# Hybrid GLA, FoX and memory block: the token norm of x moved from the activations to where projections leave PSUM

## The chip, the cores and the metric

The kernel runs on one core of a Trainium2 chip. The metric is the device time of one execution in microseconds; the figure given is the median of the runs. The engines are named as in the profile: PE is TensorE's matmul, PEld its weight load, DVE is VectorE, ACT is ScalarE, POOL is GpSimd, SP is SyncE, which issues most DMAs.

## The reference

x is 512 tokens of 1024 channels, mem 256 tokens of 1024; all is float32. One layer is computed:

```
u    = rmsnorm(x, g_mix)                 # x * rsqrt(mean(x^2) + eps) * g, per token
proj = u @ w_in                          # GLA q,k,v,gate,low-rank alpha | FoX q,k,v,forget | memory query | 3 x 1024 gates
log_a = log_sigmoid(ga @ w_alpha_up + b_alpha) / 16
o_gla = rmsnorm(gla_chunk_causal(gq/8, gk, gv, log_a), g_gla_head) * silu(gg)
o_fox = softmax(fq @ fk.T / 8 + F_t - F_s, causal) @ fv      # F = cumsum(log_sigmoid(ff + b_forget))
mk, mv = split(rmsnorm(mem, g_mem) @ w_mem_kv)
o_mem = softmax(mq @ mk.T / sqrt(128)) @ mv
merged = sum over branches of sigmoid(gate) * (o @ w_o)
h = x + merged @ w_out
h = h + relu(rmsnorm(h, g_ffn) @ w_ff1)^2 @ w_ff2
out = rmsnorm(h, g_final)
```

The norm of a token is one number, so it can be applied to u before a projection or to the projection's result.

## The kernel before, in words

Every large product is made in three matmuls: each factor is split into a high part (a cast to fp32r, on ACT) and a low part (the difference, on DVE), and `mm3` (L150) adds hi x hi, hi x lo and lo x hi in PSUM. The stationary factor is 128x128; the moving one has 512 columns, or 256 for mem. Weights come in chunks of 128x1024 in the order of `chunk_list`; `get_w` (L147) loads one on SP's queue (L136, tile raw, three buffers), casts whi (L142) and subtracts wlo (L143), three buffers each. Every second chunk also starts a DMA on POOL's queue that prepares sums of later weights (`next_sum`, L120).

`gT` (L155) is a projection with channels on partitions: eight steps of three matmuls, k over the 1024 input channels, result 128x512 in one PSUM bank, handed to an evacuation function. `gN` (L165) is a projection with tokens on partitions. Both are generators, so that `weave` (L188) can put steps of one stage as fill between steps of another. PE's order is the order of the program text; the other engines' orders are written by a scheduler at build time.

The front (L267 to L370): mem is loaded transposed, with channels on partitions, scaled by g_mem and split into mxh and mxl. The first five weight chunks are loaded and split by `lead` (L274). Four key projections of mem follow (`mk_proj`, L336), then the value projection of mem (L355, `gN`, sixteen steps). Meanwhile ACT squares mem and x, POOL and DVE add the squares over the channel slices (`sq_cols`, L206), and PE sums them over partitions with a column of ones (`rms_cols`, L218, matmuls at L224). `rsqrt` (L227) makes the norms per token: the mean on DVE, the power on POOL (L231). `bcast_rows` (L234) lays a norm out along the free axis for all partitions: ACT makes diagonal matrices (L239), PE multiplies them by ones (L240), ACT copies the result (L241). x's row rxb is then multiplied into each slice of x (L365 on POOL, L367 on DVE), and the product is split into uhi and ulo (L368). u_end is the last of these.

After the front come: G, a projection of the 16 alpha and 8 forget columns (L388); FoX queries and keys of the first head pair (`fox_pair`, L438); `decay_logs` (L396) and `decay_sums` (L408) on G's result, with FoX values as fill; the second pair; eight FoX heads (`fox_scores`, `fox_turn`, `fox_values`) woven with the other FoX and GLA projections; memory attention (L607 to L664) woven with the first gate branch; GLA (L669 to L792) woven with the second; then the third gate branch, the output projection, and from about 530 us the MLP.

`branch` (L578) makes for each of eight column blocks a gate projection, its tanh (L583) straight from PSUM, four product steps, and a combination on DVE (L596, L598). In memory attention the query of head 0 is projected first (L658); each round of the woven list then holds values of head h-2, transposes of h-1, the query projection of h+1 and scores of h, in this order. Query splits qh and ql have two buffers.

## Time and profile before

| | us |
|---|---|
| median of 3 runs | 866.18 (865.49 to 867.07) |
| profiled execution: span of its instructions | 862.5 |
| profiled execution: a time of its own beside the span | none given; the median lies 3.7 above the span |
| PE busy, and share of the span | 839.0, 97% |
| DVE busy | 542.4, 63% |
| ACT busy | 440.3, 51% |
| POOL busy | 113.0, 13% |
| mean DMA rate | 165 GB/s |

The profile is one execution. A row of the timeline gives the start in us from the span's start, the length in us, engine, line, operation, result and operands, shape, count, and in brackets the idle time before it and what ended that. A row of a stretch gives for each engine the busy time and the number of instructions, then PE's granted clock as a share of full speed, the DMA engines' busy share and GB/s. Matmul records overlap, since a matmul's last columns drain while the next one runs; the time from start to start is what a matmul costs in a dense stretch.

### The profile page before, as it was taken

What the parts mean: (1) busy time and instruction counts of PE and PEld (TensorE: products, weight loads), DVE (VectorE), ACT (ScalarE), POOL (GpSimd) and SP (SyncE); (2) the same over time, 40 slices, a digit from 0 to 9 for tenths busy, and PEclk for the clock granted to TensorE, in tenths of its full rate; (3) what the DMA queues carried; (4) which work ended last, traced back from release to release, by engine and by line L of the source; (5) the groups of instructions that cost most, each with busy time, mean ns of one, the idle gap of its engine ahead of it and who ended that gap; (6) DMA issues with size and microseconds to landing.
All of it is one profiled execution on the core that took longest, in us unless ns stands there. A gap on an engine that the chain in (4) does not pass through costs nothing.

```text
span 862.5 us, 11811 instructions
## 1 busy us (share of the span) xinstructions
PE 839.0 (97%) x4513; PEld 711.2 (82%) x4513; DVE 542.4 (63%) x850; ACT 440.3 (51%) x703; POOL 113.0 (13%) x130
## 2 busy tenths in 40 slices
PE   8999999999999999999999999999999999999993
PEld 6778788888888888787888889888997899799872
DVE  5784656756444546474533547675688678778954
ACT  7764746754333432321332436565676377457744
POOL 5100000000000021221112100111001000100234
PEclk9999999999999999999999999999999999999997
DMA  8444745544547355336222413758757956785694
GB/s 320 145 150 168 201 135 178 146 171 123 171 133 230 125 150 168 97 113 231 98 98 98 170 50 118 225 124 204 243 171 162 265 199 171 179 256 176 138 170 133
DMA packets 37513, 142.37 MB, mean 165 GB/s; under 512 B 4592, under 2 KB 5392, under 8 KB 35728
## 3 DMA queue, kind: packets, MB, share of 16 engines
q1 hardware_dynamic: 27216, 93.36, 30.5%
q0 software_dynamic: 8448, 45.09, 24.8%
q10 hardware_dynamic: 1792, 3.16, 1.1%
q8 instruction: 35, 0.57, 0.3%
q14 instruction: 22, 0.18, 0.1%
HBM read 136.34 MB, written 27.28 MB: 190 GB/s over the span
## 4 chain that ended last, share of the span: by engine, by line
PE 74%; issue 12%; DMA 6%; DVE 3%; ACT 2%; POOL 1%; SPq 0%; POOLq 0%; ACTq 0%; DVEq 0%
PE mm L152 20%; PE mm L153 20%; PE mm L151 20%; DMA b<-in_wst_dram 6%; PE a L151 2%; PE a L152 2%; PE a L153 2%; ACT hi L203 1%; PE a L748 1%; DVE lo L204 1%; PE a L477 1%; DMA cst_s<-in_cst_dram 1%; PE a L765 1%; PE a L508 1%; PE a L507 1%
## 5 line engine op out<-in xcount | busy, mean ns | idle before, releaser
L143 DVE TENSOR_TENSOR wlo<-raw,whi 128x1024 fp32r<-128x1024 f32 x80 | 101.7, 1275 | 104.1 <-ACT whi L142 103.5
L142 ACT CAST whi<-raw 128x1024 fp32r<-128x1024 f32 x80 | 84.1, 1053 | 132.3 <-PE mm L152 100.3
L151 PE MATMUL mm<-uhi,whi 128*128 128x512 f32 x360 | 142.5, 396 | 0.0
L152 PE MATMUL mm<-ulo,whi 128*128 128x512 f32 x360 | 140.7, 391 | 1.4 <-DVE ulo L204 1.4
L153 PE MATMUL mm<-uhi,wlo 128*128 128x512 f32 x360 | 140.5, 390 | 0.0
L203 ACT CAST hi<-raw 128x1024 fp32r<-128x1024 f32 x58 | 60.5, 1048 | 44.7 <-PE mm L152 31.7
L204 DVE TENSOR_TENSOR lo<-raw,hi 128x1024 fp32r<-128x1024 f32 x58 | 70.6, 1222 | 17.6 <-ACT hi L203 17.6
L152 PEld LDWEIGHTS mm<-ulo,whi 128*128 128x128 f32 x360 | 67.7, 188 | 15.8 <-DVE ulo L204 2.9
L153 PEld LDWEIGHTS mm<-uhi,wlo 128*128 128x128 f32 x360 | 67.6, 188 | 14.6 <-DVE wlo L143 0.4
L151 PEld LDWEIGHTS mm<-uhi,whi 128*128 128x128 f32 x360 | 67.7, 188 | 13.5 <-issue 0.7
L204 DVE TENSOR_TENSOR lo<-b,hi 128x1024 fp32r<-128x1024 f32 x40 | 48.9, 1223 | 38.3 <-ACT hi L203 38.2
L203 ACT CAST hi<-b 128x1024 fp32r<-128x1024 f32 x40 | 41.9, 1048 | 57.5 <-PE mm L153 24.1
L152 PE MATMUL mm<-lo,ch 128*128 128x512 f32 x160 | 63.4, 396 | 2.5 <-DVE lo L204 2.5
L151 PE MATMUL mm<-hi,ch 128*128 128x512 f32 x160 | 63.1, 395 | 0.9 <-ACT hi L203 0.8
L153 PE MATMUL mm<-hi,cl 128*128 128x512 f32 x160 | 63.0, 394 | 0.0
L1050 POOL DMA_DIRECT2D b<-in_wst_dram x32 | 27.7, 865 | 267.1 <-DVE lo L204 210.2
L152 PE MATMUL mm<-u2l,hi 128*128 128x256 f32 x192 | 54.3, 283 | 0.0
L153 PE MATMUL mm<-u2h,lo 128*128 128x256 f32 x192 | 54.3, 283 | 0.0
L151 PE MATMUL mm<-u2h,hi 128*128 128x256 f32 x192 | 54.3, 283 | 0.0
L151 PE MATMUL mm<-u2sh,hi 128*128 128x256 f32 x144 | 40.8, 283 | 0.0
L152 PE MATMUL mm<-u2sl,hi 128*128 128x256 f32 x144 | 40.8, 283 | 0.0
L153 PE MATMUL mm<-u2sh,lo 128*128 128x256 f32 x144 | 40.8, 283 | 0.0
(349 smaller groups left out, 1945.5 us busy)
## 6 DMA issues: line engine op xcount, KB each, us to landing
raw<-in_wst_dram SPq DMA_DIRECT2D x122, 512.0 KB, 4.0
b<-in_wst_dram POOLq DMA_DIRECT2D x32, 512.0 KB, 5.3
T<-in_wst_dram POOLq DMA_DIRECT2D x12, 1024.0 KB, 8.4
raw<-T SPq DMA_DIRECT2D x24, 512.0 KB, 4.5
b<-in_wst_dram SPq DMA_DIRECT2D x16, 512.0 KB, 5.1
xr<-in_xT_dram SPq DMA_DIRECT2D x4, 512.0 KB, 8.1
nFb<-dF ACTq DMA_DIRECT2D x8, 256.0 KB, 3.8
h<-in_xN_dram SPq DMA_DIRECT2D x4, 512.0 KB, 7.6
```

Of the source, the lines that this page charges most:

```text
L142: cast = nc.scalar.copy(hi, raw)
L143: nc.vector.tensor_tensor(lo, raw, f(hi), op=ALU.subtract)
L151: nc.tensor.matmul(ps, lh, rh, start=start, stop=False)
L152: nc.tensor.matmul(ps, lh, rl, start=False, stop=False)
L153: nc.tensor.matmul(ps, ll, rh, start=False, stop=stop)
L203: nc.scalar.copy(hi, src)
L204: return nc.vector.tensor_tensor(lo, src, f(hi), op=ALU.subtract).ins
L477: nc.tensor.matmul(ps[:, :w], q, K[e][:, 1, :w], start=False, stop=True)
L507: nc.tensor.matmul(po[:, q0:], vv, PTh[:, c0:c0 + w], start=n == 0, stop=False)
L508: nc.tensor.matmul(po[:, q0:], vv, PTl[:, c0:c0 + w], start=False, stop=n == 3)
L748: nc.tensor.matmul(ps[:, t, :], kk[:, sl], qq[:, sl], start=True, stop=True)
L1050: nc.gpsimd.dma_start(to, x, accum_op=ALU.add)
```

## The change

- uhi and ulo are made from x times g_mix, without the token norm. The row rxb lives on through the layer, and every projection's result is multiplied by it (tokens along the free axis) or by the column rtok (tokens on partitions) where it leaves PSUM: G, FoX q, k and v, GLA q, k, v and gate, and the 24 gate blocks. The memory query is split unscaled; its scores take the norm in the softmax's scale (rpos) and maximum (rneg).
- The sums of squares are taken from copies of x and mem in token order, loaded on POOL's queue after the last split of mem: two of mem, four of x, 512 KB each, through two buffers (nat). ACT squares and sums in one instruction, or DVE does. `sq_cols` and `rms_cols` are gone. The broadcast of mem's norm stands after six of the value steps, that of x's norm after four of the eight steps of G.
- The first key projection is a plain f32 product of unsplit weights (w0) with unsplit mem times g_mem (mg); mxh and mxl are made from mg.
- Three small constants are made on POOL instead of DVE; key evacuations of mem go to DVE.
- In FoX a strip of the tile ab is used for scaled results (ev_t) and another for th. In memory attention qh and ql have one buffer, and scores of h stand ahead of the query projection of h+1.

The diff, cut to its core:

```diff
@@ rsqrt: takes r; sq_cols and rms_cols removed @@
+    rtok, rneg, rpos = (cst_s[:, 4 * P + 8 * i:4 * P + 8 * i + NT] for i in range(3))
...
+    rxb = up.tile([P, S], F32, name="rxb")
@@ front @@
+        mg = [sg[k // 2][:, (k % 2) * M:(k % 2) * M + M] for k in range(KT)]
+        def lead(key, tag):
+            raw = (wp if tag == "raw" else fp).tile([P, 1024], F32, tag=tag, name=nm("raw"), bufs=3 if tag == "raw" else 2)
+            pre[key] = [wp.tile([P, 1024], F32R, tag=g, name=nm(g)) for g in ("hi", "lo")]
+            nc.sync.dma_start(raw, wst[index[key]])
+            split(*pre[key], raw)
...
+        w0 = wp.tile([P, 1024], F32, tag="raw", name=nm("raw"))
         for j in range(4):
             nc.sync.dma_start(memr[:, 2 * j:2 * j + 2], memT[:, 2 * j:2 * j + 2])
+            nc.sync.dma_start(w0[:, 256 * j:256 * j + 256], wst[0][:, 256 * j:256 * j + 256])
             for k in (2 * j, 2 * j + 1):
-                nc.scalar.mul(mxh[:, k, :], memr[:, k, :], gmem[:, k:k + 1])
-                nc.vector.scalar_tensor_tensor(mxl[:, k, :], memr[:, k, :], gmem[:, k:k + 1], f(mxh[:, k, :]),
-                                               op0=ALU.mult, op1=ALU.subtract)
-                if k == 2 * j:
-                    lead(chunks[0], 4, j)
+                nc.vector.tensor_scalar(mg[k], memr[:, k, :], gmem[:, k:k + 1], None, op0=ALU.mult)
+            for k in (2 * j, 2 * j + 1):
+                last_mx = nc.scalar.copy(mxh[:, k, :], mg[k])
+                nc.vector.tensor_tensor(mxl[:, k, :], mg[k], f(mxh[:, k, :]), op=ALU.subtract)
...
+        def natural(src, to, on_act):
+            nat = fp.tile([P, D], F32, tag="nat", name=nm("nat"), bufs=2)
+            d = nc.gpsimd.dma_start(nat, src)
+            tc.add_manual_dep(d.ins, last_mx.ins.name, ..., reason="pace")
+            if on_act:
+                nc.scalar.activation(nat, nat, AF.Square, accum_out=to)
+            else:
+                nc.vector.tensor_tensor_reduce(out=nat, in0=nat, in1=nat, scale=1.0, scalar=0.0, op0=ALU.mult, op1=ALU.add,
+                                               accum_out=to)
+        for t in range(2):
+            natural(memN[t * P:(t + 1) * P, :], msum[:, t:t + 1], True)
+        rm = rsqrt(fp, msum, 1.0 / D, 2)
...
         for k in range(KT):
-            sq_cols(fp, memr, M, k, macc, range(KT), "m")
+            nc.scalar.mul(uhi[:, k, :], xr[:, k, :], gmix[:, k:k + 1])
+            u_end = nc.vector.scalar_tensor_tensor(ulo[:, k, :], xr[:, k, :], gmix[:, k:k + 1], f(uhi[:, k, :]),
+                                                   op0=ALU.mult, op1=ALU.subtract).ins
+        nc.gpsimd.tensor_copy(ident16, ident)
+        nc.gpsimd.tensor_scalar(cmask, tri, -1.0, -NEG, op0=ALU.add, op1=ALU.mult)
+        msk_end = nc.gpsimd.tensor_copy(msk_s.rearrange("p a b -> p (a b)"), cst_s[:, 4 * P:6 * P])
+        for t in range(NT):
+            natural(xN[t * P:(t + 1) * P, :], xsum[:, t:t + 1], t % 2 == 0)
+        rsqrt(fp, xsum, 1.0 / D, NT, rtok)
+        nc.vector.tensor_scalar(rpos, rtok, float(P) ** -0.5, None, op0=ALU.mult)
+        nc.vector.tensor_scalar(rneg, rtok, -float(P) ** -0.5, None, op0=ALU.mult)
...
+        ps = mmt()
+        for k in range(KT):
+            nc.tensor.matmul(ps[:, :M], w0[:, k * P:(k + 1) * P], mg[k], start=k == 0, stop=k == KT - 1)
+        nc.vector.tensor_copy(mk_raw(0), ps[:, :M])
+        for h in range(1, 4):
+            mk_proj(h)
+        mv = gN([("N", "w_mem_kv", 2 * j, 512) for j in range(4)], of(mxh, mxl), 2, mmt, mv_evac)
+        run(islice(mv, 6))
         bcast_rows(fp, rm, M, rmb)
-        mk_proj(3)
...
-        rx = rms_cols(fp, xacc, S)
...
-        bcast_rows(fp, rx, S, rxb)
-        for k in range(KT):
-            ut = fp.tile([P, S], F32, tag="ut", name=nm("ut"), bufs=3)
-            if k in UP:
-                nc.gpsimd.tensor_tensor(ut, xr[:, k, :], rxb, op=ALU.mult)
-            else:
-                nc.vector.scalar_tensor_tensor(ut, xr[:, k, :], gmix[:, k:k + 1], rxb, op0=ALU.mult, op1=ALU.mult)
-            u_end = split(uhi[:, k, :], ulo[:, k, :], ut)
         run(mv)
+        g_steps = gT(("G",), uhi, ulo, lambda ps: ga_evac(ps))
+        run(islice(g_steps, 4))
+        bcast_rows(fp, rtok, S, rxb)
@@ FoX and GLA projections @@
-            nc.scalar.copy(gaT, ps)
+            nc.vector.tensor_tensor(gaT, ps, rxb, op=ALU.mult)
...
+        abf = ab.rearrange("p t c -> p (t c)")
+        ev_t, th_t = abf[:, 0:S], abf[:, S:2 * S]
+        def scaled(to, ps, c=None):
+            if c is None:
+                nc.vector.tensor_tensor(to, ps, rxb, op=ALU.mult)
+            else:
+                nc.vector.scalar_tensor_tensor(to, ps, c, rxb, op0=ALU.mult, op1=ALU.mult)
...
             def q_evac(ps):
+                scaled(ev_t, ps, 0.125)
                 for e, a, b in rows:
-                    nc.scalar.mul(Q[a, e, :], ps[a], 0.125)
-                    nc.vector.scalar_tensor_tensor(tq[a], ps[a], 0.125, f(Q[a, e, :]), op0=ALU.mult, op1=ALU.subtract)
+                    nc.scalar.copy(Q[a, e, :], ev_t[a])
+                    nc.vector.tensor_tensor(tq[a], ev_t[a], f(Q[a, e, :]), op=ALU.subtract)
             def k_evac(ps):
+                scaled(ev_t, ps)
                 for e, a, b in rows:
-                    split(K[e][a, 0, :], K[e][a, 1, :], ps[a])
+                    split(K[e][a, 0, :], K[e][a, 1, :], ev_t[a])
...
-            return proj(OFF["gk"] + P * j, lambda ps: nc.scalar.copy(gkT[j], ps))
+            return proj(OFF["gk"] + P * j, lambda ps: scaled(gkT[j], ps))
@@ gates @@
-            nc.scalar.activation(th, ps, AF.Tanh, scale=0.5)
+            nc.vector.tensor_tensor(th, ps, rxb, op=ALU.mult)
+            nc.scalar.activation(th, th, AF.Tanh, scale=0.5)
@@ memory attention @@
-                st["q", h] = [ap.tile([P, S], F32R, tag=g, name=nm(g), bufs=2) for g in ("qh", "ql")]
+                st["q", h] = [ap.tile([P, S], F32R, tag=g, name=nm(g)) for g in ("qh", "ql")]
...
-                nc.vector.tensor_scalar(m2, m2, -sc, None, op0=ALU.mult)
+                nc.vector.tensor_tensor(m2, m2, rneg[:, 2 * g:2 * g + 2], op=ALU.mult)
...
-            for fn, i in ((mem_values, h - 2), (mem_turn, h - 1), (lambda i: run(mem_q(i)), h + 1), (mem_scores, h)):
+            for fn, i in ((mem_values, h - 2), (mem_turn, h - 1), (mem_scores, h), (lambda i: run(mem_q(i)), h + 1)):
```

95 lines of the change are left out of this document (28 added, 67 removed).

## The prediction

> **What bounds the kernel now.** I read first the page's busy shares and the table of stretches of 20 us, then the PE timeline and the waits of the one region where TensorE is not full, and last single rows of the places further on that the change touches.
>
> ```profile
> span 862.5 us, 11811 instructions
> PE 839.0 (97%) x4513; PEld 711.2 (82%) x4513; DVE 542.4 (63%) x850; ACT 440.3 (51%) x703; POOL 113.0 (13%) x130
> ...
> 0.00:20.00 20.00, 16.11 (x79) 11.42 (x80) 10.91 (x18) 15.70 (x35) 10.54 (x15) 0.91 0.87 312
> 20.00:40.00 20.00, 19.04 (x113) 16.52 (x113) 15.02 (x19) 14.24 (x25) 2.97 (x4) 1.00 0.49 173
> 40.00:60.00 20.00, 18.64 (x79) 14.06 (x78) 17.33 (x27) 11.84 (x21) 2.04 (x3) 1.00 0.35 121
> 60.00:80.00 20.00, 20.00 (x91) 16.26 (x90) 8.74 (x23) 11.73 (x17) 1.23 (x2) 1.00 0.52 185
> ```
>
> In the stretches, the second number after each start is TensorE's (PE's) busy time. PE is busy 97% of the span, and from 60 us on it is full. The first 60 us lack 20.00 - 16.11, 20.00 - 19.04 and 20.00 - 18.64, together 6.2 us, and busy time there hides more, since matmuls overlap. So two things can move the time: how soon PE gets through the front, and any new wait in the full part, where a stall of PE costs its whole length.
>
> The front on PE, from the timeline (start, length, line, operands; in brackets the idle time before and who ended it):
>
> ```profile
> 14.34 0.58 PE L153 MATMUL mm<-mxh,lo 128*128 128x256 f32 x1
> ...
> 24.46 0.39 PE L151 MATMUL mm<-hi,mxh 128*128 128x512 f32 x1
> 25.55 0.50 PE L152 MATMUL mm<-lo,mxh 128*128 128x512 f32 x1 [0.69 <-DVE lo L284]
> 26.82 1.84 PE L224 MATMUL a<-cst_s,acc 128*128 128x1 f32 x16
> 28.52 0.49 PE L151 MATMUL mm<-hi,mxh 128*128 128x512 f32 x1
> 32.07 0.60 PE L240 MATMUL a<-dg,cst_s 128*128 128x128 f32 x4
> ...
> 33.48 0.48 PE L151 MATMUL mm<-whi,mxh 128*128 128x512 f32 x1
> ...
> 39.73 0.39 PE L151 MATMUL mm<-uhi,whi 128*128 128x512 f32 x1
> ...
> 42.90 0.50 PE L152 MATMUL mm<-ulo,whi 128*128 128x512 f32 x1 [0.74 <-DVE ulo L204]
> ```
>
> At 14.34 the second key projection for mem begins to flow, at 24.46 the value projection for mem, at 26.82 the sums of squares of x by matmul (1.70 us to 28.52), at 32.07 the broadcast of x's norm (1.41 us to 33.48), at 39.73 the chunk called G, the first to read u. From 33.48 to 39.73 stand nine steps of three matmuls, 6.25 us: 0.231 us each. The row at 42.90 shows what G waits for: ulo, which comes only after norm, product and split of each slice of x.
>
> **The change part by part.** The sum is made against the profiled execution. The profile gives its span, 862.5 us, and no other time of its own; the median, 866.18, lies 3.7 us above, which I take as unchanged launch and end.
>
> *The norm leaves u's path.* The eight products with the norm (L367, L365) go; uhi and ulo are made straight from x, which is long in SBUF, while the mem projections run. G has eight steps, 24 x 0.231 = 5.5 us. The first matmul of the next projection:
>
> ```profile
> 47.50 0.40 PE L151 MATMUL mm<-uhi,whi 128*128 128x512 f32 x1
> ```
>
> From 39.73 to 47.50 it took 7.8 us, so 2.2 us go. What hides the eight casts and eight subtractions is the stretch 24 to 40, where the other engines have room:
>
> ```profile
> 12.00:16.00 4.00, 3.31 (x14) 3.02 (x15) 3.95 (x4) 3.70 (x8) 3.44 (x3) 0.58 1.03 416
> 16.00:24.00 8.00, 8.00 (x69) 8.00 (x69) 4.42 (x6) 6.96 (x14) 3.78 (x4) 1.00 1.01 394
> 24.00:40.00 16.00, 15.04 (x80) 12.52 (x79) 11.38 (x16) 10.56 (x18) 2.38 (x3) 1.00 0.37 119
> ```
>
> (Columns: PE, PEld, DVE, ACT, POOL, then PE's granted clock, DMA share, GB/s.) Beside 16.0 us VectorE (DVE) has 11.4 and ScalarE (ACT) 10.6. If that cover were gone, G would stall as now.
>
> *Sums of squares on PE go:* 1.7 us for x, and for mem a quarter as many instructions, 0.4 us. The broadcast of the norm stays (1.4 us), only later, among G's steps. G is long enough to cover the copy of the row to SBUF.
>
> *The first key projection* becomes eight plain f32 products without a split. It waits on loads as before; I cost it at nothing. The next projection waited at 14.34 for its lo part:
>
> ```profile
> 12.20 3.75 DVE L284 TENSOR_TENSOR lo<-raw,hi 128x256 fp32r<-128x256 f32 x3
> 6.11 0.73 POOL L216 TENSOR_TENSOR acc<-acc,sq 128x256 f32<-128x256 f32 x1 [4.84 <-ACT sq L215]
> 12.40 5.39 POOL L216 TENSOR_TENSOR acc<-acc,sq 128x256 f32<-128x256 f32 x4 [0.61 <-ACT sq L215]
> 23.20 1.04 ACT L283 CAST hi<-raw 128x1024 fp32r<-128x1024 f32 x1
> ```
>
> Three subtractions took 3.75 us while GpSimd (POOL) added squares, four of them 5.39 us, 1.35 each, where one at 6.11 took 0.73. Two engines that stretch each other here no longer meet; I take 0.6 us for it, between 0 and 1.1. The clock of 0.58 from 12 to 16 us (the row above) may stay; were it 1.00, 4 x 0.42 = 1.7 us would be won. I keep that for the lower end. The sum of the gains: 2.2 + 1.7 + 0.4 + 0.6 = 4.9 us.
>
> *New loads in a full stretch.* Two copies of mem and four of x in token order, 0.52 MB each, 3.1 MB, go out on POOL's queue. From 12 to 24 us the DMA share is about 1.0 at 394 to 416 GB/s: there the copies of mem alone cost 1.05 MB / 0.41 = 2.6 us to whatever queues beside them. That is:
>
> ```profile
> 9.23 0.33 SPq L282 DMA_DIRECT2D raw<-in_wst_dram  x1
> 11.26 0.43 SPq L282 DMA_DIRECT2D raw<-in_wst_dram  x1
> 11.74 0.43 SPq L315 DMA_DIRECT2D cst_s<-in_cst_dram  x1
> DMA to landing us min/median/max: 5.1/5.9/7.2
> xr<-in_xT_dram SPq DMA_DIRECT2D x4, 512.0 KB, 8.1
> b<-in_wst_dram POOLq DMA_DIRECT2D x32, 512.0 KB, 5.3
> b<-in_wst_dram SPq DMA_DIRECT2D x16, 512.0 KB, 5.1
> ```
>
> (Issues of the weight chunks of the fourth key projection and of the first value step, and of the masks' constants; then the us to landing of all eight early chunk loads, and in the page's rows KB and median us to landing.) With the longest, 7.2 us, the first chunk lands at 16.4 and the second at 18.5 now; 2.6 us later, 19.0 and 21.1; hi and lo take 1.04 + 1.2 us more, so ready at 21.3 and 23.4. PE wants the first at 24.46 less 24 half-width matmuls of 0.12, less the 0.6 and 0.4 won above and 0.4 for mem's broadcast, which moves behind it: 20.1; its third matmul needs lo, so some 1.0 us of stall. It wants the second at 24.0 and waits only if copies of x are in front too; I take 0.4, where now 0.9 is lost (the row at 25.55). New loss 1.0 + 0.4 - 0.9 = 0.5 us. The ends: a gain of 0.9, if POOL's descriptors come late and the weights pass first; a loss of 3, if two copies of x as well, 2.6 us more, get ahead of the second chunk.
>
> *The norm of x by its copies.* Four loads share two buffers, so the second pair waits for the squares of the first. If POOL casts the masks first, whose constants land by the 8.1 us of the last x loads at 19.8, now 22.4, the first pair goes at about 22.5. A round is 0.9 us for two issues (0.43 each on SP), 5.3 to landing, 1.2 of squares (the 1024-wide ACT pass above took 1.04; reading out the sum is my allowance of 0.2). Two rounds end at 37.3, then 0.2 for the mean and the power on POOL:
>
> ```profile
> 28.94 1.03 POOL L231 TENSOR_TENSOR rr<-ms,cst_s 128x4 f32<-128x4 f32 x1 [8.35 <-DVE ms L230]
> ```
>
> That is 38.5 us, and ScalarE makes the first diagonal 0.4 us later, 38.9. PE wants it after four of G's steps: 24.4, sixteen value steps of 0.69, 0.4 for mem's own broadcast, four steps of 0.69, 38.6. So 0.3 us of stall; lower end 0, the upper end is a rival. The front wins 4.9 - 0.5 - 0.3 = 4.1 us.
>
> *The order of memory queries and scores.* Scores of head 0 now follow its own query projection at once, since the loop puts the next projection behind the scores and qh, ql have one buffer. Today a whole projection covers the split. The rows where it is made (PE's last matmul of that projection, then ACT, DVE):
>
> ```profile
> 221.56 0.39 PE L153 MATMUL mm<-uhi,wlo 128*128 128x512 f32 x1
> 222.03 0.58 ACT L203 CAST qh<-mm 128x512 fp32r<-128x512 f32 x1
> 222.16 1.23 DVE L143 TENSOR_TENSOR wlo<-raw,whi 128x1024 fp32r<-128x1024 f32 x1 [2.97 <-ACT whi L142]
> 223.31 0.68 DVE L204 TENSOR_TENSOR ql<-mm,qh 128x512 fp32r<-128x512 f32 x1
> ```
>
> The next matmul could start at 221.78. ql is there at 223.99, because VectorE takes the next weights' lo first. PE can do two short matmuls meanwhile, 0.24 us: 2.0 us of stall, in the full part, at full price. The lower end is 0.58 + 0.68 = 1.3, were ql ahead of the weights; the upper 2.2. I take 2.0, the order of the rows. Later heads have a projection and fill between and cost nothing.
>
> *Scaling at the PSUM exit* adds some 36 passes of 128x512 on VectorE (24 gates, 8 FoX queries and keys, 4 gate columns of GLA) and moves 4 from ScalarE. The price is that of the subtraction at 223.31, 0.68 us for the same size out of PSUM. The places with least slack:
>
> ```profile
> 68.33 0.19 DVE L405 TENSOR_TENSOR lf<-lf,ab 128x32 f32<-128x32 f32 x1 [3.89 <-ACT ab L404]
> 70.15 0.30 PE L411 MATMUL a<-lf,cst_s 128*128 128x32 f32 x2
> 99.81 0.73 PE L491 MATMUL a<-cst_s,Pt 128*128 128x128 f32 x2 [0.24 <-DVE Pt L484]
> 389.69 0.88 DVE L750 COPY_PREDICATED at<-msk_s,a 128x128 f32<-128x128 uint8 x4
> 390.98 0.44 PE L763 MATMUL a<-gv,at 128*64 128x128 f32 x4
> ```
>
> Of 40 x 0.68 = 27.2 us nearly all lies beside PE: between 60 us and the end VectorE has that much room, and a gate has 12 matmuls of the branch's product behind it before its tanh is wanted. Three places do not have it. At 68.5 the forget logs are ready, PE takes them at 70.15: 1.6 us of slack, into which go a scaling pass, and the wait of ab for the reads of the strip that is now laid over it. I take 0.3, between 0 and 1.5. At 99.81 PE waits for the first head's softmax already; a scaling of the next keys on VectorE and a later cast on ScalarE push the chain by one pass, 0.7, between 0 and 1.4. At 389.69 + 0.88 the GLA mask ends 0.4 us before PE takes it; a gate's pass falls there: 0.3, and with its like at other heads 0.4, between 0 and 1.5. Sum of losses in the full part: 2.0 + 0.3 + 0.7 + 0.4 = 3.4 us.
>
> **The sum:** 862.5 - 4.1 + 3.4 = 861.8 us of span, 866.18 - 0.7 = 865.5 us of time: the front wins, and the later stages hand most of it back.
>
> **Weighed with the Trainium skill.** In this stretch POOL's work is stretched by VectorE's, 0.73 to 1.35 us above, but loads on POOL's queue land in 5.3 us beside 5.1 on SP's. The Trainium skill, SBUF — State Buffer, section "SBUF: two separate sides", says that a load issued by GpSimd needs it to write descriptors through the port pair shared with VectorE, and gives 620 ns alone against 3100 ns beside a two-port VectorE operation. As an estimate from that page, 2.5 us on each of two rounds of x loads would make the norm 5 us later and the time about 870. The landing rows do not show it; the first rows in which GpSimd loads meet a busy VectorE in the front will be those of the changed kernel.
>
> **The rivals.**
> *The weights pass unhurt.* POOL's loads find gaps, or start late, and the clock holds. For it: after 24 us the DMA moves only 119 GB/s; against it: the stretch before is full. The front then wins 4.9 to 7.5 us (with the clock's 1.7 and the 0.9 at 25.55), less 3.4: 862.1 to 864.7, typically 863.4. Chance 0.28.
> *The norm of x comes late.* The place is the broadcast inside G. Loads of 8.1 us to landing, as x's own took in the full stretch, instead of 5.3, make two rounds of 10.2 us from 22.5; the first diagonal stands at 44.5, 5.9 us behind PE, 5.6 more than counted: 871.1. From a norm at about 41 us on the change is slower by more than can be mistaken. The rule of the page above would be one way to it. For it: the two buffers, the long queue behind the masks; against it: the DMA has room after 24 us. Chance 0.19, 868 to 872.
> *u is still late,* though the norm is out of it: x lands by 19.8, and eight casts of 0.6 and eight subtractions of 0.68 have until 35.8; I give it nothing.
> *VectorE becomes the limit in the late stages*, each tight place at its upper end: up to 3.0 us more than the 1.4 taken: 868 to 869. Chance 0.05, since between 60 and 80 us it is busy for 8.74 of 20 us.
>
> **How the numbers follow.** The forecast has 0.48, own range 863.5 to 868. About 0.2%, 1.7 us, is what a measurement of this kernel tells from no change, so the marks are 864.4 and 867.9. Of the forecast's 0.48 I put 0.06 below, 0.38 between, 0.04 above; of the first rival's 0.28, 0.27 below and 0.01 between; the second's 0.19 is above; of the third's 0.05, 0.02 between and 0.03 above. Faster 0.33, same 0.41, slower 0.26. The range 862.3 to 869.8 leaves out the best of the first rival and the worse half of the second, some 0.15.
>
> **What would show it.** Right, if G takes about 7.4 us with its only pause at the broadcast and ends near 43 instead of 47.5 us; if no matmul waits for ulo; if PE stands still about 2 us between the first memory query projection and the first memory scores; if nothing else past 60 us waits over 1 us. Wrong, if G's broadcast waits for POOL's power (second rival), if the value projection runs without a wait for lo and the clock stays at 1.00 (first), or if ql is split ahead of the weights.

## The result and the profile after

| | before | after |
|---|---|---|
| median of the runs made side by side, us | 866.18 (863.35 to 868.94, 7 runs) | 870.83 (869.67 to 876.22, 7 runs) |
| profiled execution: time, span, mean granted clock | span 862.5, clock 0.990 | 876.22, span 874.4, clock 0.981 |

The change makes the kernel slower: the ratio is 1.0078, 95% interval 1.0054 to 1.0101, some 6.7 us (the two medians alone lie 4.7 apart). The forecast was 865.5 us with a range to 869.8; the measured time lies outside it, on the side of the second rival ("the norm of x comes late", 868 to 872). The profiled execution after lies 5.4 us above its median; the other six have spans of 867.9 to 873.0 us. The profiled execution of one variant (a1) took 2420 us at a mean clock of 0.338, so its trace is not used.

The page's busy shares after:

```profile
span 874.4 us, 11754 instructions
PE 841.4 (96%) x4485; PEld 713.1 (82%) x4485; DVE 562.5 (64%) x892; ACT 436.8 (50%) x680; POOL 105.1 (12%) x128
```

DVE is busy for 20 us more on balance: the scaling passes have come, the products with the norm and the sums of squares have gone. PE's waits after (us in total, times, longest):

```profile
PE a L221 <- ACT dg L220: 3.9, 1, 3.9
PE mm L153 <- DVE lo L205: 3.3, 6, 0.8
PE mm L152 <- ACT hi L204: 3.0, 2, 1.9
PE a L489 <- DVE Pt L482: 1.6, 2, 1.3
...
PE a L152 <- ACT qh L204: 1.4, 1, 1.4
...
PE a L154 <- DVE ql L205: 0.9, 1, 0.9
```

No matmul waits for ulo any more, as forecast. In its place stand a wait of 3.9 us for the diagonal of x's norm (dg), 1.6 at the first turn of FoX (Pt), and 1.4 + 0.9 at the first memory scores (qh, ql). The stretches of the front, and two short ones further on (columns as in the prediction: PE, PEld, DVE, ACT, POOL, PE's granted clock, DMA share, GB/s):

```profile
12.00:20.00 8.00, 6.52 (x50) 6.11 (x50) 6.49 (x9) 5.23 (x7) 1.96 (x3) 1.00 1.02 410
20.00:27.00 7.00, 3.90 (x24) 3.37 (x25) 5.22 (x9) 6.28 (x10) 2.12 (x4) 0.92 1.03 401
27.00:33.00 6.00, 6.00 (x16) 4.62 (x15) 2.78 (x3) 3.03 (x5) 0.80 (x2) 0.53 0.91 317
...
40.00:47.40 7.40, 3.51 (x16) 2.58 (x14) 4.72 (x9) 4.40 (x9) 1.35 (x3) 0.93 0.74 247
47.40:53.40 6.00, 5.91 (x18) 4.80 (x19) 0.00 (x0) 1.66 (x4) 0.00 (x0) 0.52 0.00 1
...
108.00:111.40 3.40, 3.40 (x13) 2.98 (x14) 1.72 (x3) 1.57 (x4) 0.00 (x0) 0.54 0.70 231
234.00:237.40 3.40, 3.40 (x13) 2.82 (x12) 1.54 (x4) 1.46 (x5) 0.00 (x0) 0.51 0.47 190
```

The clock column is the second news. Behind each of the new stalls PE runs at about half clock for 3.4 to 6 us: 27 to 33 (after the wait for the first value chunk of mem), 47.4 to 53.4 (after the wait for dg), 108 to 111.4 (after Pt), 234 to 237.4 (after qh and ql). A matmul that costs 0.23 us at full clock costs 0.43 there, so six such microseconds, were they full of such matmuls, would lose 2.8, and 3.4 lose 1.6.

How x's norm came so late, from the timeline (start, length; in brackets idle time and what ended it):

```profile
21.84 1.04 ACT L295 ACTIVATE nat<-nat 128x1024 f32<-128x1024 f32 x1
23.27 0.53 POOL L291 DMA_DIRECT2D nat<-in_xN_dram  x1 [9.31 <-ACT nat L295]
25.04 1.05 ACT L295 ACTIVATE nat<-nat 128x1024 f32<-128x1024 f32 x1
26.48 0.57 POOL L291 DMA_DIRECT2D nat<-in_xN_dram  x1 [1.12 <-ACT nat L295]
33.34 0.60 PE L221 MATMUL a<-dg,cst_s 128*128 128x128 f32 x4
33.98 0.37 ACT L222 COPY gv<-a 128x256 f32<-128x256 f32 x1 [1.34 <-PE a L221]
34.25 1.06 ACT L295 ACTIVATE nat<-nat 128x1024 f32<-128x1024 f32 x1
35.70 0.58 POOL L291 DMA_DIRECT2D nat<-in_xN_dram  x1 [7.86 <-ACT mkh L204]
35.74 1.22 DVE L297 CUSTOM_DVE_ANT_0 nat<-nat 128x1024 f32<-128x1024 f32 x1
37.27 0.53 POOL L291 DMA_DIRECT2D nat<-in_xN_dram  x1 [0.99 <-DVE xsum L297]
42.87 1.06 ACT L295 ACTIVATE nat<-nat 128x1024 f32<-128x1024 f32 x1
44.23 1.22 DVE L297 CUSTOM_DVE_ANT_0 nat<-nat 128x1024 f32<-128x1024 f32 x1
45.89 1.05 POOL L212 TENSOR_TENSOR cst_s<-ms,cst_s 128x4 f32<-128x4 f32 x1 [8.10 <-DVE ms L211]
47.42 2.51 PE L221 MATMUL a<-dg,cst_s 128*128 128x128 f32 x8 [3.91 <-ACT dg L220]
...
54.08 0.39 PE L152 MATMUL mm<-uhi,whi 128*128 128x512 f32 x1
```

And from the page's DMA part (KB each, median us to landing):

```profile
nat<-in_xN_dram POOLq DMA_DIRECT2D x4, 512.0 KB, 4.7
```

The first two copies of x are sent for at 23.27 and 26.48, each when ScalarE has squared a copy of mem (21.84, 25.04) that held one of the same two buffers, and land in 4.7 us. Their squares run only at 34.25 and 35.74: ScalarE and VectorE work in order, and ahead of the squares stand the copy of mem's norm (33.98, which waits for PE's broadcast at 33.34) and the key scalings behind it. ScalarE stood idle for 1.34 us ahead of that copy, with the landed square next in its queue. Until then both buffers are taken, so the other two copies leave at 35.70 and 37.27. PE has done four of G's steps at 43.35; the norm is there at 46.94. The last row is the first matmul of the next projection: G ends at 54.08.

Start times of the same work in the traces:

| us | before | after | a2 late broadcast | c1 both | c4 copies later | c5 key ahead |
|---|---|---|---|---|---|---|
| first value step of mem | 24.46 | 25.19 | 24.38 | 24.86 | 22.16 | 21.33 |
| G | 39.73 | 40.63 | 39.21 | 39.03 | 37.06 | 36.35 |
| decay projection | 58.63 | 64.98 | 56.45 | 56.27 | 54.62 | 54.41 |
| decay sums | 70.15 | 76.30 | 67.76 | 67.58 | 65.94 | 65.72 |
| first FoX scores | 93.89 | 100.02 | 91.50 | 91.30 | 89.66 | 94.90 (one projection more ahead) |
| first product with FoX output | 233.44 | 246.98 | 235.23 | 232.25 | 232.25 | 228.25 |
| first GLA decays | 317.62 | 331.10 | 319.35 | 316.78 | 316.78 | 312.77 |
| second MLP product | 568.34 | 581.82 | 570.07 | 567.49 | 567.50 | 563.49 |

After is 6.35 us behind at the decay projection, 13.54 at the first product with FoX output, and keeps 13.48 from GLA to the second MLP product. (At PE's last matmul it is 10.7, 859.20 against 848.48: the profiled execution before has a half-clock stretch of its own near 830 us.) In parts: 0.9 at G, 5.4 more by the decay projection, 0.2 less by the first FoX scores, 7.4 more by the first product.

### The profile page after: what moved, and what is told of

It is laid out like the page before. It is cut to its first block, busy times and chain, and to the rows that moved or that the text cites. A ratio compares the mean times of both kernels' runs of the same rounds, so it can differ in the third digit from the quotient of the medians.

```text
span 874.4 us, 11754 instructions
## 1 busy us (share of the span) xinstructions
PE 841.4 (96%) x4485; PEld 713.1 (82%) x4485; DVE 562.5 (64%) x892; ACT 436.8 (50%) x680; POOL 105.1 (12%) x128
## 4 chain that ended last, share of the span: by engine, by line
PE 71%; issue 12%; DMA 9%; ACT 3%; DVE 2%; POOL 1%; SPq 0%; POOLq 0%; ACTq 0%; DVEq 0%
PE mm L153 19%; PE mm L152 19%; PE mm L154 19%; DMA b<-in_wst_dram 6%; PE a L154 2%; PE a L153 2%; PE a L152 2%; DVE lo L205 1%; DMA xr<-in_xT_dram 1%; ACT hi L204 1%; DMA h<-s 1%; PE a L750 1%; POOL h L1052 1%; PE a L475 1%; DMA raw<-in_wst_dram 1%
## 5 line engine op out<-in xcount | busy, mean ns | idle before, releaser
L152 PE MATMUL mm<-uhi,whi 128*128 128x512 f32 x360 | 144.4, 401 | 0.0
L205 DVE TENSOR_TENSOR lo<-raw,hi 128x1024 fp32r<-128x1024 f32 x62 | 75.6, 1224 | 19.2 <-ACT hi L204 19.2
L204 ACT CAST hi<-raw 128x1024 fp32r<-128x1024 f32 x62 | 64.6, 1048 | 46.4 <-PE mm L153 31.7
```

The costliest lines, as they stand in the source:

```text
L152: nc.tensor.matmul(ps, lh, rh, start=start, stop=False)
L204: nc.scalar.copy(hi, src)
L205: return nc.vector.tensor_tensor(lo, src, f(hi), op=ALU.subtract).ins
```

## The experiments

Ratios are to the kernel before, run beside each on the same chip. All but b1 are built on the changed kernel.

### The late norm: a2_late_broadcast and e1_nat4

a2 moves G's exit and the broadcast of x's norm behind the first seven steps of the next projection:

```diff
-        run(islice(g_steps, 4))
-        bcast_rows(fp, rtok, S, rxb)
...
+        run(islice(pair, 6))
+        # four diagonals in separate strips, then ones x diagonal, copy, exit of G
+        ga_exit(held_g[0])
```

> The changed kernel with G's exit and the broadcast of x's norm moved behind seven of the eight steps of the first FoX query projection, the four diagonals in four separate strips. PE would ask for the norm at about 49 us instead of 43.4; it was ready at 47.0. Theory A: the stall of 4.3 us, some 1.4 us of waiting between the diagonals, and up to 4 us of half clock go: 5 to 8 us faster than the changed kernel, 863 to 866. Theory B: 4.5 to 5.5 us faster, near 866. Rival C (loads): the norm's lateness is only a sign of it; less than 2 us faster, above 869.

Measured 865.17 us, ratio 0.9996 (0.9983 to 1.0009). PE no longer waits for dg, and between 40 and 60 us it is full at full clock:

```profile
40.00:60.00 20.00, 20.00 (x94) 16.75 (x93) 12.04 (x19) 12.31 (x22) 1.91 (x4) 1.00 0.53 178
```

The decay projection starts at 56.45, 2.2 us ahead of before, not 6.35 behind. So the late norm costs 7.1 us at the median (1.0078 less 0.9996, of 866), and 8.5 in the two traces, of which 1.4 had arisen ahead of G (40.63 against 39.21). From G to the decay projection it takes 24.35 us after and 17.24 in a2; in a3 and a5, whose front is that of the change, 23.44 and 23.37. That makes 6.1 to 7.1. The time lies in theory A's range and next to theory B's figure; the trace has no stall here and so can't tell what the half clock costs.

e1 changes one size, the buffers for the copies from two to four:

> One size of the changed kernel is altered: the tile into which the token-order copies are loaded has four buffers in place of two. Theory (queue and buffers): in the changed kernel the third and fourth copy of x were only sent for at 35.70 and 37.27 us, because the first two sat in their buffers until ScalarE and VectorE, in order, came to square them at 34.25 and 35.74. With four buffers all four are sent for before 30 us, the last square ends near 38.5, the norm is there near 40, and the four broadcast matmuls inside G find it (they were reached at 43.35): no wait of PE for dg, no half clock after it, the decay projection at 56 to 59 us in place of 64.98, and a ratio to the kernel before of 0.998 to 1.002 in place of 1.0078. Rival (the loads themselves are slow, or the squares stand behind other work in any case): the fourth square still ends after 43 us, PE waits over 2 us for dg, ratio 1.006 to 1.010.

Measured 869.11 us, ratio 1.0045 (1.003 to 1.006). The theory holds for the norm and fails for the time:

```profile
26.50 1.04 ACT L204 CAST hi<-raw 128x1024 fp32r<-128x1024 f32 x1 [2.13 <-DMA raw<-in_wst_dram]
27.60 0.80 PE L152 MATMUL mm<-hi,mxh 128*128 128x512 f32 x1 [4.44 <-ACT hi L204]
36.98 1.22 DVE L297 CUSTOM_DVE_ANT_0 nat<-nat 128x1024 f32<-128x1024 f32 x1
39.77 1.86 POOL L212 TENSOR_TENSOR cst_s<-ms,cst_s 128x4 f32<-128x4 f32 x1 [9.05 <-DVE ms L211]
45.01 0.60 PE L221 MATMUL a<-dg,cst_s 128*128 128x128 f32 x4
```

The last square runs at 36.98, the norm is there at 41.6, and the broadcast at 45.01 finds it (a wait of 0.27 us stays). But two copies of x now leave near 13 us, into the stretch that moves 410 GB/s; they land in 9.6 us at the median by the page, the first value chunk of mem lands late, and PE waits 4.44 us for its hi in place of 1.90. The norm is there 6.6 us after the start of mem's broadcast on PE (34.99), where after the change it takes 13.6 (33.34 to 46.94). That the queues and the two buffers made the norm late is thus shown; that more buffers would mend it is not: the wait moved to the weights.

### The order of memory scores: a1_mem_order, b1_mem_order_alone, a3_fill_stall, c1_both

a1 puts the former order back into the changed kernel; b1 puts the new order into the kernel before.

```diff
-            for fn, i in ((mem_values, h - 2), (mem_turn, h - 1), (mem_scores, h), (lambda i: run(mem_q(i)), h + 1)):
+            for fn, i in ((mem_values, h - 2), (mem_turn, h - 1), (lambda i: run(mem_q(i)), h + 1), (mem_scores, h)):
```

(With it, two buffers for qh and ql as before, and in a1 one for the softmax weights Pm, to make room.)

> The changed kernel with the memory query of the next head projected ahead of the scores again, qh and ql with two buffers (room comes from one buffer for the probabilities instead of two). Theory A (a stall of PE costs its length and, when the granted clock halves after it, about 1.7 us more for 3.4 us at half clock): the 2.9 us stall ahead of the first memory scores goes, and the half-clock stretch behind it: about 4.5 us faster than the changed kernel, near 866.3. Theory B (a stall costs its length alone): 2.0 to 2.9 us faster, near 868.3. Rival C (the loads of the copies in the front are the loss, and PE's later stalls are made up elsewhere): no change, 870.8.

> The kernel before with this one part of the change alone: scores of a head ahead of the next head's query projection, one buffer for qh and ql. Theory A: 2.0 us of stall and about 1.7 us of half clock more: 3.5 to 4.5 us slower than before, near 870. Theory B: 2.0 us slower, near 868.2. Rival C: no change.

a1 measured 868.6 us, ratio 1.0040 (1.0027 to 1.0053), 3.3 us better than the change, between the two theories and nearer to B. b1 measured 869.38, ratio 1.0052 (1.0040 to 1.0065): the order by itself costs 4.5 us, as theory A has it. The two runs don't decide between the theories. In b1's trace the distance to before is 0.72 us ahead of the memory scores and 5.06 behind them, and from 226 to 229.4 us the granted clock is 0.50. The place in the trace after:

```profile
230.04 0.39 PE L154 MATMUL mm<-uhi,wlo 128*128 128x512 f32 x1
231.19 0.58 ACT L204 CAST qh<-mm 128x512 fp32r<-128x512 f32 x1
231.32 1.22 DVE L144 TENSOR_TENSOR wlo<-raw,whi 128x1024 fp32r<-128x1024 f32 x1 [3.08 <-ACT whi L143]
231.82 0.39 PE L152 MATMUL a<-mkh,qh 128*128 128x256 f32 x1 [1.39 <-ACT qh L204]
232.46 0.68 DVE L205 TENSOR_TENSOR ql<-mm,qh 128x512 fp32r<-128x512 f32 x1
233.20 0.39 PE L154 MATMUL a<-mkh,ql 128*128 128x256 f32 x1 [0.87 <-DVE ql L205]
```

In a2, where the clock stayed at 1.00 here, the stretch from the query's last matmul (219.88) to the first behind the scores (224.32) took 4.44 us; dense, twelve short matmuls and that last one take 1.67. The stall's own price is 2.8 us; the rest of b1's 4.3 and of after's 4.4 is the half clock behind it.

a3 fills the stall with twenty dead matmuls, to hold the clock up:

```diff
+        pw = at_()
+        for _ in range(20):
+            nc.tensor.matmul(pw[:, :256], ident16, cb_s.rearrange("p a b -> p (a b)"), start=True, stop=True)
```

> The changed kernel with 20 bf16 matmuls of 256 columns, read by nobody, put on PE between the first memory query projection and the first memory scores, about 2.1 us of the 2.9 us stall. The wait stays as long; only PE is not idle in it. Theory A: the granted clock stays at 1.00 behind it, 1 to 1.7 us faster than the changed kernel where that one is slowed, 869 to 870. Theory B: 870.8, no change, and the clock rows alike.

Measured 872.21 us, ratio 1.0087 (1.0069 to 1.0105): no gain. Its profiled execution held full clock there, and the same stretch took 4.45 us, but so it did in a2 and a5, which have the stall without the filler. The filler helps nothing that can be measured.

c1 joins a2 and the former order:

> The late broadcast and the former order of the memory attention together (second query projection ahead of the first scores, two buffers for the split queries, one for the memory weights). Theory (the terms add): 0.9996 for the late broadcast less 0.0038 (1.0078 less 1.0040, what the former order gave back): 0.996, 862.0 us where the kernel before has 865.6; the memory stage loses nothing (2.8 us at full clock in the late-broadcast run), what is left of the front's gain is 2.4 us and what is left of loss is 1.4 us at the first turn of FoX. Rival (the stall at the memory scores was paid in any case, for instance by the clock): 0.999 to 1.000.

Measured 862.87 us, ratio 0.9974 (0.9959 to 0.9990): faster than both kernels, though less so than the sum of the two (0.996). The former order is worth 1.9 us here, 3.3 on the change, 4.5 alone.

### The first turn of FoX: d1_fox_unscaled, c2_pool_copies, c5_key_ahead

d1, on c1, leaves the norm out where FoX queries and keys leave PSUM:

```diff
-                scaled(ev_t, ps)
                 for e, a, b in rows:
-                    split(K[e][a, 0, :], K[e][a, 1, :], ev_t[a])
+                    split(K[e][a, 0, :], K[e][a, 1, :], ps[a])
...
```

> As the kernel with the late broadcast and the former memory order, but the FoX queries and keys leave PSUM as in the kernel before, without the norm of the token (that part of the computation is left out here). It asks what the scaling pass ahead of each split costs at the first turn of FoX, where PE waited 1.62 us for the weights Pt. Theory (the pass on VectorE puts off the key copies and they come between the exponentials): no wait over 0.3 us there, from the first FoX scores to the last matmul of the first memory query 127.0 us as in the kernel before (128.4 with the passes), ratio 0.0016 below the kernel with both: about 0.994. Rival (the order of the exponentials comes from something else): the wait stays, and the ratio equals that of the kernel with both within 0.0005.

Measured 861.04 us, ratio 0.9949 (0.9930 to 0.9969): 2.2 us below c1. The wait for Pt is 0.2 us, and from the first FoX scores to the first memory scores it takes 136.64 us, as before the change (136.73); with the passes 138.14. The place, in the trace after:

```profile
100.22 0.69 DVE L384 TENSOR_TENSOR ab<-mm,rxb 128x512 f32<-128x512 f32 x1 [2.04 <-PE mm L154]
100.99 1.25 ACT L204 CAST K<-ab 64x512 fp32r<-64x512 f32 x2
102.26 1.28 ACT L479 ACT_TABLE_LOAD   x1
...
105.17 1.05 ACT L452 CAST K<-K 64x1024 fp32r<-64x1024 f32 x1
106.24 0.72 ACT L479 ACTIVATE Pt<-Pt,mx 128x512 f32<-128x512 f32 x1
107.82 0.48 PE L489 MATMUL a<-cst_s,Pt 128*128 128x128 f32 x1 [1.33 <-DVE Pt L482]
```

The second key of FoX is scaled at 100.22, so its casts stand on ScalarE ahead of the table load, and a key copy (105.17) stands ahead of the last exponential. c2 moves these copies to GpSimd (`nc.gpsimd.tensor_copy` for `nc.scalar.copy`):

> As the kernel with the late broadcast and the former memory order (0.9974), but the second halves of the FoX keys (two copies of 64x1024, 1.04 us each on ScalarE, 96.65 and 98.56 us in the late-broadcast run) are copied by GpSimd. Theory (these copies stand between the exponentials and hold back the weights that the first turn waits for): the wait of 1.6 us for Pt falls below 0.5, from the first FoX scores to the last matmul of the first memory query 127.0 to 127.4 us, ratio 0.9950 to 0.9960. Rival (the scaling pass itself, or GpSimd is slow enough that a later head's scores wait for the copied keys): the wait stays over 1 us or a new wait for K of as much appears, ratio 0.9970 or above.

Measured 862.36 us, ratio 0.9973 (0.9959 to 0.9987), the same as c1; a wait of 1.26 us for Pt stays, in one piece. Not the copies alone, then. c5 leaves all norms in and moves a GLA key projection ahead of the first scores (on c4, below):

```diff
-        weave(steps, 128, gla_k(0), gla_k(1), ...
+        run(gla_k(0))
+        weave(steps, 120, gla_k(1), ...
```

> The kernel with the later copies (0.9971), all norms applied, and the first GLA key projection (24 matmuls, 5.5 us of PE, one pass of VectorE at its exit) is moved ahead of the first FoX scores, so that the scaled exit of the second FoX key lies beside it and no longer between the first scores and their turn. Theory (the scaling pass and the splits behind it hold VectorE and ScalarE just when the first weights Pt are wanted): the wait of 1.6 us for Pt falls below 0.5 and ratio 0.9940 to 0.9955. Rival (the exit of the key moved ahead, its weight split of 1.05 and 1.22 us, takes the same place, or a later turn stalls with 8 fewer fill steps): a wait of over 1 us for Pt stays, ratio 0.9965 to 0.998.

Measured 858.71 us, ratio 0.9929 (0.9902 to 0.9955), the fastest of all and below the range expected of it. Nothing waits for Pt; the scaled key now leaves beside a full PE:

```profile
89.66 0.69 DVE L389 TENSOR_TENSOR ab<-mm,rxb 128x512 f32<-128x512 f32 x1 [2.04 <-PE mm L154]
92.41 2.12 ACT L457 CAST K<-K 64x1024 fp32r<-64x1024 f32 x2 [0.72 <-DVE K L205]
95.94 1.28 ACT L484 ACT_TABLE_LOAD   x1
98.72 0.71 ACT L484 ACTIVATE Pt<-Pt,mx 128x512 f32<-128x512 f32 x1
100.11 0.60 PE L494 MATMUL a<-cst_s,Pt 128*128 128x128 f32 x4
```

So the stall came from the place of the scaled key's exit, among the first head's exponentials: it goes when the scaling goes (d1) and when the exit comes earlier (c5).

### The size of the front's gain: a4_no_copies, c3_squares_later, c4_copies_later, d2_later_unscaled

a4 fills the copies' tiles with ones in place of the six loads:

```diff
-            d = nc.gpsimd.dma_start(nat, src)
-            tc.add_manual_dep(d.ins, last_mx.ins.name, ..., reason="pace")
+            nc.gpsimd.memset(nat, 1.0)
```

> The changed kernel with its six loads of token-order copies left out: each tile is filled with ones by GpSimd in place of the load, and squared and summed as before (the norms are then those of ones). It asks what the loads do to the front by themselves. Theory (their 3 MB delay the weight chunks): the wait of 1.90 us for hi of the first memory value chunk and of 0.80 for lo goes below 1 us together, the memory values start no later than 24.0 (25.19 changed, 24.46 before), the norm is there before 43 us, the decay projection at 53 to 56 us, ratio 0.997 to 1.000. Rival (that chunk is late for another reason, the order of ScalarE and VectorE behind the splits of u): the wait for hi and lo stays above 2 us, the decay projection at 56 to 59, ratio 0.999 to 1.002.

Measured 866.07 us, ratio 1.0010 (0.9994 to 1.0026). G's broadcast waits 0.3 us, the decay projection starts at 56.36; but the value steps start at 26.85, since with the copies at hand a square was put ahead of a lo that PE waits 2.5 us for, and from 16 to 24 us the granted clock is 0.70. The rival's numbers came out, not by the rival's cause; the copies' traffic is not told apart by it.

c3, on c1, puts mem's two squares behind u's splits in the program:

> As the kernel with the late broadcast and the former memory order (0.9974), but the two squares of mem's copies are put behind the eight splits of u in the program. In the former PE waited 1.89 us for hi and 0.82 us for lo of the first memory value chunk, and ScalarE squared a copy at 21.51 (1.23 us with its read-out) shortly ahead of that hi at 23.77. Theory (ScalarE's order is what makes hi late): hi comes 1.2 us sooner, the two waits fall to 1.5 us or less together, the memory values start at 23.7, the decay projection at 55 or sooner (56.27), ratio 0.9955 to 0.9965. Rival (the last parts of x or the chunk itself land late, so that hi can't go sooner): hi stays within 0.4 us of 23.77, ratio 0.997 to 0.998.

Measured 861.89 us, ratio 0.9969 (0.9958 to 0.9981), c1 again. The scheduler put the square where it was, at 21.36 ahead of hi at 23.63, so the question stayed unasked. c4 also sends for the copies later:

```diff
+            cu = nc.scalar.mul(uhi[:, k, :], xr[:, k, :], gmix[:, k:k + 1])
+            if k == 5:
+                last_mx = cu          # the copies wait for the sixth split of u, not the last of mem
...
-        run(islice(mv, 6))
+        run(islice(mv, 12))
         bcast_rows(fp, rm, M, rmb)
```

> As the kernel with mem's squares behind the splits of u, and besides all token-order copies are only sent for when ScalarE has split the sixth part of u (near 20 us in place of 12), and mem's broadcast matmuls stand after 12 of the 16 steps of the memory values in place of 6. Theory (from 12 to 24 us the transfers run at 410 GB/s with all queues busy, and mem's two copies, 1 MB, stand for 2.6 us of that ahead of x and the weight chunks): u and the chunk come up to 2.6 us sooner, the memory values start at or before 23.0, PE waits under 1 us for their hi and lo and has no half clock from 27 to 33, the decay projection at 52 to 54.5, ratio 0.992 to 0.995. Rival (hi is late by ScalarE's order, or the chunks are called up no sooner): memory values start after 24, decay projection 55.5 to 56.5, ratio 0.9965 to 0.998.

Measured 862.23 us, ratio 0.9971 (0.9960 to 0.9983). The front does what the theory said: value steps at 22.16 (24.86 in c1), no half clock from 24 to 36, decay sums 4.2 us ahead of before. The time does not: at the first turn of FoX, with the same stall of 1.62 us, c4 drops to half clock and c1 does not. c1, then c4:

```profile
97.00:100.00 3.00, 1.67 (x11) 1.23 (x12) 1.05 (x4) 2.88 (x6) 0.00 (x0) 1.00 1.05 242
100.00:103.00 3.00, 3.00 (x15) 2.48 (x15) 2.31 (x4) 1.87 (x4) 0.00 (x0) 1.00 0.48 186
```

```profile
97.00:100.00 3.00, 2.53 (x12) 2.18 (x13) 1.96 (x4) 2.11 (x4) 0.00 (x0) 0.75 1.01 302
100.00:103.00 3.00, 3.00 (x11) 2.37 (x10) 0.91 (x3) 1.05 (x1) 0.00 (x0) 0.68 0.05 16
```

d2 is c4 with d1's edit, to see whether the 4.2 us stay once that stall is gone:

> The kernel with the later copies (0.9971), and FoX queries and keys leave PSUM without the norm of the token (that part of the computation is left out). In the run with the later copies the front was 4.2 us ahead of the kernel before at the first FoX scores (1.8 to 2.6 in its sisters) but only 1.2 ahead at the memory scores: the stall of 1.6 us at the first turn was followed by half clock from 97 to 103 us, which none of its sisters had there. Theory (the front's gain is real and the stall at the turn with its half clock gives it back): with that stall gone the 4.2 us stay to the second product, ratio 0.9930 to 0.9940. Rival (the clock takes back elsewhere what the front gains, or the ratio is bound by a stream of its own): the ratio of the kernel with earlier copies and unscaled FoX, 0.9949, or above, with a new stretch of half clock or a wait ahead of the memory scores.

Measured 860.80 us, ratio 0.9948 (0.9928 to 0.9968), d1's 0.9949. The rival's figure, in an unforeseen place: in this execution the half clock fell at 12 to 20 us, and the front was 2.7 us ahead, not 4.2.

```profile
12.00:20.00 8.00, 6.83 (x43) 6.63 (x44) 5.75 (x8) 6.81 (x10) 0.21 (x1) 0.79 1.02 407
```

### The gates: a5_gates_unscaled

a5 leaves the scaling of the first two branches' gates out (tanh reads PSUM):

> The changed kernel with the 16 scaling passes of the two branches' gates left out (tanh reads PSUM as in the kernel before; the gates then lack the norm of the token). Theory (VectorE has room in these stages, from 231 to 520 us no wait of PE was added): no change against the changed kernel, 1.0065 to 1.0090 (1.0078). Rival (the passes hold PSUM or ScalarE back by some tenths each): 1.005 or less, and the distance from the first GLA decays to u2 under 192.0 us (192.11 before and after the change).

Measured 872.59 us, ratio 1.0100 (1.0076 to 1.0124): no gain; four runs, and an interval that covers the range expected. The distance named there was wrong: from the first GLA decays to the MLP it is 205.59 us before, after, and in a5 alike. The gates' passes cost nothing that shows.

## Why the prediction was wrong

By the ratios, one step at a time from the change back: former memory order (a1) 3.3 us; late broadcast on top (c1) 5.7; FoX queries and keys unscaled on top (d1) 2.2. What is left stands 4.4 us ahead of before. So 3.3 + 5.7 + 2.2 - 4.4 = 6.8, the measured loss; this closes by construction, each step being the difference of two ratios, and what ties a step to its place is the wait that goes with it in the traces. The order of steps matters: the other way round the broadcast is worth 7.1 and the memory order 1.9. Each figure is uncertain by one to two microseconds.

- **"That is 38.5 us", the norm of x: forecast 0.3 us, measured 5.7 to 7.1.** The step that failed. The sum let each square run as soon as its copy had landed. But ScalarE and VectorE work in order, and ahead of the squares stands the work on mem's norm, which waits for PE's broadcast of it at 33.34: that cost six microseconds between the landing near 28 (23.27 + 4.7) and 34.25, and through the two buffers was handed on to the second pair. "Two rounds end at 37.3" became 45.45. The norm thus hangs on PE itself. In all eight traces with this order and two buffers (after, a2, a3, a5, c1, c2, c3, d1) it is there 13.6 us after the start of mem's broadcast, and PE after the change needs 10.0 from there to its own request (33.34 to 43.35). The wait is the rest, with the first diagonal: 3.91 after the change, and 3.91 in a3 and a5, whose fronts run at other times. That PE came at 43.35 and not at 38.6 hid nothing, since the same delay moved both.

  G took 13.45 us (40.63 to 54.08) in place of the 7.4 that were to show the forecast right: PE stood for 4.1, the broadcast took 2.2 in place of 1.4, and at half clock the last twelve matmuls took 4.49 where the first twelve took 2.72. The landing was about right (5.3 forecast, 4.7). The first issue was too (22.5, 23.27), but by luck: it did not stand behind the masks, which come after it (24.23 and 24.63), it waited for a buffer until mem's first square was done; and the second left 3.2 us behind it, not half a microsecond.

  The second rival had the place, and its time of 871.1 lies by the measured 870.83, but not the cause: it took slow loads. That the times agree is partly luck, since other stages took a share of the loss. The Trainium skill, SBUF — State Buffer, section "SBUF: two separate sides", says that a load issued by GpSimd stands still, without its descriptors, while VectorE in a two-port operation holds the port pair that they share. The landing of 4.7 us, below the 5.4 of the weight loads on the same queue in this trace, shows nothing of it.
- **"I take 2.0, the order of the rows", memory scores: 2.8 without the clock, 4.4 with it;** by the ratios 1.9 to 4.5. The order of rows was right (qh, then the weights' lo, then ql). The row I took for the projection's last matmul was not it: the scores stand 42 matmuls of 0.227 us behind the projection's end, which puts it at 220.88, not 221.56, and qh starts 1.15 us behind it, as after (230.04 to 231.19). That is 0.7 us. The other 1.6 is the half clock, of which the prediction had nothing.
- **"One pass, 0.7", the first turn of FoX: 1.4 without the clock, 3.0 with it;** 2.2 between the ratios of c1 and d1. The bound of 1.4 held for the stall. I counted the pass on VectorE, not the key copy that it pushes between two exponentials.
- **"0.3" for the decay sums and "0.4" for GLA: nothing.** From the decay projection to the sums it takes 11.32 us after, 11.52 before; from GLA's first decays on the distance stays at 13.48. The passes lie beside PE, as a5 shows for the gates.
- **"4.1 us", the front, 4.4 without the norm's stall: 1.8 to 4.4 in the traces.** G's waits for ulo and the sums on PE are gone. With the late norm out of the way the decay sums start 1.8 to 3.5 us ahead of before where a stretch of the front runs at half clock (a2, c1, c2, c3, d1, d2) and 4.2 to 4.4 where none does (c4, c5); the ratios of d1 and d2, which take in the whole execution, show 4.4, with an interval of 2.7 to 6.1. Inside it, "new loss 0.5" was too low after the change: PE waits 1.90 for the first value chunk's hi and 0.80 for its lo, where 0.69 stood before, and half clock follows. With the copies sent for later (c4) the wait for hi and the half clock are gone; 1.45 for lo stays.
- **The first rival's clock.** The stretch from 12 to 16 us did run at 1.00 after, as it said; the half clock came at 27 us instead.

Not settled: which stall is followed by half clock in a given execution. c1 and c4 have the same 1.62 us at the same place, and only c4 pays. The nine traces with those two pieces of stall at the first turn (0.29 and 1.33 us) lose the clock in three (after, a4, c4); the six with the unfilled stall at the memory scores in four (after, a4, b1, e1); the three with 3.91 us at G in all three (after, a3, a5). A profile shows one execution of each kernel; how the price is shared out over all of them can't be told from here. That c1 and c4 agree in time while their profiled executions lose the clock in different places fits it, and does not prove it.

## What to carry to other kernels

When work is moved off a critical product, time what replaces it by its place in each engine's in-order queue and by the buffers its loads share, not by its own length: a 1 us square behind a copy that waits for PE came 6 us late and held up the next load as well. Look for a loop in particular: here PE waited for a norm whose squares waited for PE, and the wait stayed at 3.91 us whether the front came early or late. In a stream that is otherwise full, price a stall of two microseconds at its length, and in the range at up to 1.6 us more for the 3.4 us of half clock that may follow. A scaling at an exit is free where nobody waits and dear between a softmax and its first reader; there a projection put between (c5, 858.71 us with every norm applied) was worth 3.6 us (0.9971 to 0.9929).

## What the hardware showed

- In the profiled execution after, stalls of 1.6 us (first turn, in two pieces of 0.29 and 1.33) and of 2.3 (memory scores) were each followed by 3.4 us at a granted clock of 0.51 to 0.54, and the 3.9 us at G by 6 us at 0.52; in a2, a3, a5, c1, c3 and e1 the same 1.6 us left the clock at 1.00. The Trainium skill, TensorE: Matmul & The Clock Gate, section "HAM oscillation — how this bites in real kernels", gives the rule as no idle gaps over some 3.4 us. Here shorter ones sufficed, at times.
- From 12 to 24 us 16 DMA engines carried 400 to 411 GB/s in every trace used here. Two copies of 512 KB more in that stretch (e1) put the copies' landing from 4.7 to 9.6 us and PE's wait for a weight chunk from 1.90 to 4.44.
